# A two-block transformer step on one core: the low part of the stream moved beside its high part in the dense products

## The chip, the core and the metric

The kernel runs on one core of one Trainium2 chip. The core has a matrix engine (TensorE, PE in the profile, with its weight loads shown apart as PEld), a vector engine (VectorE, DVE), a scalar engine (ScalarE, ACT), a slower elementwise engine (GpSimd, POOL) and a queue that issues transfers (SyncE, SP). The metric is the device time of one execution in microseconds (us), median of several runs.

## The reference, cut to what matters

Two transformer blocks over 256 positions of width 1024, all in float32. The first has a layer of gated causal attention with 16 heads ("fox"), a feed-forward, a layer of latent attention with 8 heads ("mla") and a second feed-forward. The second has a mixer (a spatial gating unit beside differential attention), cross-attention into 256 memory tokens, and a mixture of 32 experts. The part that the change touches is a chain of dense products with a nonlinearity, such as

```python
def sq_relu_mlp(h, w_up, w_down):
    return jnp.square(jax.nn.relu(h @ w_up)) @ w_down

x = x + fox_mixer(rms_norm(x, g0), ...)        # q, k, v products, 16 heads, output product
x = x + sq_relu_mlp(rms_norm(x, g1), w_up, w_down)   # 1024 -> 4096 -> 1024, twice
x = x + mla_mixer(...)                          # low-rank products, 8 heads, output product
z = rms_norm(x, g2) @ w_in                      # second block: u, v, q, k and values
x = x + memory_attention(...)
x = x + hierarchical_moe(...)
```

## The kernel before, in words

The stream is held feature-major: 8 chunks of 128 features on the partitions, 256 positions in the free dimension. To keep float32 accuracy with fast products, every operand is split in two float32r parts: the high part is the value rounded to float32r, the low part is what the rounding left. A product of one weight block of 128x128 with one chunk of the stream is then three matmuls of 256 columns into the same 256 columns of a PSUM bank (`mm3`, L454 to L456): high weight with high stream, high weight with low stream, low weight with high stream.

The weights come as a planned sequence of slices. Most slices are 128x1024: eight 128x128 blocks that together give 128 output features, so eight `mm3` calls, 24 matmuls. A ring of SBUF tiles receives the slices by DMA; `prep` (L419, L425) splits a slice: ACT casts the high part (128x1024), DVE subtracts for the low part. `take` calls `prep` so that three slices ahead are split (`NSPLIT = 4`); the low part is issued one call late, at the next `prep` or `flush`. So the program order on ACT is, for each slice: cast of a later slice, then what evacuates this slice's PSUM bank; on DVE: subtraction of a later slice, then its share of the evacuation. Each engine runs its instructions in this program order.

`proj` takes one slice, draws one of the two banks tagged `pp`, issues its `mm3` calls and returns the bank. The caller evacuates it, in `fox` with one DVE multiplication by the row of reciprocal norms (L855, L859), in `ffn` with four instructions (L942 to L945): ACT relu, ACT square into the high part `hh`, DVE square, DVE subtraction into the low part `hl`. The third slice in a row has to wait until the first one's bank is evacuated.

The dense slices come in this order: 8 for the memory keys (mk), wide ones with 512 moving columns (mv, fv: `proj_wide`, L462 to L464, whose stationary operand is the stream), 16 for fox (fk, fq), 8 output (fo), then the feed-forward in four blocks of 8 `up` and 8 `down` slices; then qa 3, kva 3, kb, qn, qr, vb of mla, 8 output (mo), the second feed-forward; then sv (wide), su 4, dk and dq 4 each around a wide dv, 8 output (wo), 8 mq, 8 om. `out_proj` adds the bank of an output slice to the stream (`finish_x`, L917) and makes the next normalised operand from it (L513, L514).

Attention work is put between the slices by a small pipe: each `pipe.step()` issues the next stage of the heads under way (scores L641, softmax L597 and L599, normalise L606 or L1223 and L1225, transpose L612, values). In the `up` part of a block nothing but the slices runs. At the first `up` slice of a feed-forward the reciprocal norm is computed (L537 on PE, L573 and L575 on ACT, L578 to L580 and L556 on DVE) ahead of that slice's evacuation. In `second`, two ACT gelu instructions on `vt` (L1189) stand ahead of the evacuation of the first su slice.

The last third of the time is the mixture of experts, which reads three tiles of 128x4096 float32 for each expert.

Of the kernel before, what the change touches and what calls it, by code (L numbers as in the profile page):

```python
# [303 lines left out]

class Program:
# [151 lines left out]

    def mm3x(self, out, xh, xl, w, o, n, start, stop):
# [44 lines left out]
    def pair(self, name, n=8, pool=None):  # L503
        return tuple(self.t(name + part, [128, n, 256], F32R, pool=pool) for part in "hl")
# [201 lines left out]
    def memory_keys(self, memx):  # L706
# [14 lines left out]
        for m in range(8):  # L721
# [68 lines left out]
    def fox(self):  # L790
# [58 lines left out]
        for c in range(8):  # L849
# [8 lines left out]
            p = self.proj("fq", xn)  # L858
            nc.vector.scalar_tensor_tensor(q, p, 0.125, rb, op0=OP.mult, op1=OP.mult)  # L859
# [14 lines left out]
    def out_proj(self, key, ctx, norms, k2=0, order=range(8), post=None, mid=None, between=None, ahead=2):  # L874
# [3 lines left out]
        first = []  # L878
        if k2:
            oldest = self.used  # L880
            groups, n = k2 if isinstance(k2, tuple) else (k2,), 0
            for a, b in zip((0, *groups), groups):
                for m in range(ahead):
                    if a == 0:
                        first.append((self.bank("pp" if m < 2 else "ps", [128, 256]), self.take(key, oldest)))
                    p, w = first[m]
                    for i in range(a, b):
                        k = order[i]
                        self.mm3(p, w, k * 128, 128, ctx[0][:, k], ctx[1][:, k], i == 0, False)
# [6 lines left out]
        for m in range(8):  # L896
            if m < len(first):
                p, w = first[m]
            else:
                p, w = self.bank("pp", [128, 256]), self.take(key)  # L900
            for i in range(k2 if m < len(first) else 0, 8):
                k = order[i]
                self.mm3(p, w, k * 128, 128, ctx[0][:, k], ctx[1][:, k], i == 0, i == 7)
            if post and m > 1:
                post(m - 2)
            self.finish_x(m, p, norms, split=post and m == 7)
# [21 lines left out]
    def ffn(self, layer, norms, final=False):  # L928
# [6 lines left out]
        for b in range(4):  # L935
            for f in range(8):
# [17 lines left out]
            for m in TURNS if b == 3 else range(8):  # L954
# [7 lines left out]
                if b == 3:  # L962
                    t = self.t("rs", [128, 256], bufs=2)
                    nc.vector.tensor_mul(t, o, r2)
                    self.finish_x(m, t, [(n, self.nxt[n]) for n in self.nxt])
# [19 lines left out]
    def mla(self):  # L985
# [8 lines left out]
        for part in (range(0, 6), range(6, 8)):  # L994
            for c in range(3):
                if part[0] == 0:
                    late.append(self.bank("acc", [128, 256]))
# [887 lines left out]
```

## Time and profile before

| | before |
|---|---|
| median of 3 runs (lowest, highest) | 1271.92 us (1270.92, 1272.26) |
| the profiled execution's own time | 1270.38 us |
| its span, first to last instruction | 1268.7 us |
| PE busy, weight loads | 1198.2 us, 966.5 us |
| DVE busy, ACT busy, POOL busy | 661.2 us, 525.0 us, 156.0 us |
| DMA moved | 338.63 MB |

Busy times are unions of instruction intervals over the span. A matmul's interval is its latency, and consecutive matmuls overlap; the pace of PE is read from the starts of consecutive matmuls, not from their durations. "Idle before <- X" names what an engine's instruction waited for last.

### The profile page before, as it was taken

The page shows a single profiled execution, that of the slowest core. Times are in us where ns is not written, and L with a number is a line of the kernel's source. Part 1 is how long each engine was busy: PE and PEld are TensorE (multiplying, and loading weights), DVE is VectorE, ACT ScalarE, POOL GpSimd, SP SyncE. Part 2 cuts the span into 40 slices and gives each one's busy share as a digit, 9 for nine tenths or more (in the row PEclk, how much of TensorE's full clock was granted, in tenths as well). Part 3 has the DMA queues.
Part 4 walks back from the last instruction along what each step waited for, and adds up shares of the span by engine and source line. Part 5 has one row for each costly group of instructions (what it writes and reads, how often), then busy time and mean ns, then how long its engine had stood idle before and what let it go on. Part 6 is the DMA issues. An engine that isn't in the chain of part 4 may idle for free. (4 is left out here: it accounts for less than half of the span.)

```text
span 1268.7 us, 22238 instructions
## 1 busy us (share of the span) xinstructions
PE 1198.2 (94%) x9282; PEld 966.5 (76%) x9282; DVE 661.2 (52%) x1249; ACT 525.0 (41%) x980; POOL 156.0 (12%) x169
## 2 busy tenths in 40 slices
PE   8999999999999999999999999988999999787886
PEld 7788899999998899999998898854554545444333
DVE  7657675654787574654789775432222223222222
ACT  4555564544654664544665554221112122121212
POOL 5166110000032010000145110100000000000000
PEclk9999999999999999999999999998999999898997
DMA  9554435545442345544554358899999999999995
GB/s 347 198 211 153 169 133 200 192 163 204 173 165 94 133 142 192 199 169 172 191 211 184 134 199 346 318 378 427 424 426 425 427 424 425 427 424 425 426 421 205
DMA packets 30520, 338.63 MB, mean 267 GB/s; under 512 B 3521, under 2 KB 3793, under 8 KB 8401
## 3 DMA queue, kind: packets, MB, share of 16 engines
q1 hardware_dynamic: 30272, 336.92, 66.8%
q8 instruction: 74, 1.21, 0.4%
q10 hardware_dynamic: 144, 0.26, 0.1%
q14 instruction: 30, 0.24, 0.1%
HBM read 336.10 MB, written 1.06 MB: 266 GB/s over the span
## 5 line engine op out<-in xcount | busy, mean ns | idle before, releaser
L425 DVE TENSOR_TENSOR wl<-ring,wh 128x1024 fp32r<-128x1024 f32 (+1 forms) x244 | 302.9, 1246 | 73.6 <-ACT wh L419 73.6
L419 ACT CAST wh<-ring 128x1024 fp32r<-128x1024 f32 (+1 forms) x246 | 252.6, 1030 | 140.7 <-PE acc L455 95.8
L454 PE MATMUL pp<-xh,wh 128*128 128x256 f32 x800 | 227.3, 284 | 0.1
L455 PE MATMUL pp<-xl,wh 128*128 128x256 f32 x800 | 225.9, 282 | 0.4 <-DVE xl L514 0.4
L456 PE MATMUL pp<-xh,wl 128*128 128x256 f32 x800 | 225.9, 282 | 0.0
L455 PE MATMUL acc<-hl,wh 128*128 128x256 f32 x560 | 159.3, 284 | 1.6 <-DVE hl L514 1.0
L456 PE MATMUL acc<-hh,wl 128*128 128x256 f32 x560 | 158.5, 283 | 0.9 <-DVE wl L425 0.9
L454 PE MATMUL acc<-hh,wh 128*128 128x256 f32 x560 | 158.7, 283 | 0.0
L454 PEld LDWEIGHTS pp<-xh,wh 128*128 128x128 f32 x800 | 151.6, 189 | 2.2 <-issue 1.6
L455 PEld LDWEIGHTS pp<-xl,wh 128*128 128x128 f32 x800 | 150.3, 188 | 0.8 <-DVE xl L514 0.6
L456 PEld LDWEIGHTS pp<-xh,wl 128*128 128x128 f32 x800 | 150.1, 188 | 0.0
L1644 PE MATMUL pp<-ring,xg 128*32 128x512 f32 x1024 | 125.9, 627 | 21.2 <-DMA ring<-in_we_dram 18.3
L530 POOL TENSOR_TENSOR sq<-sq,sqt 128x256 f32<-128x256 f32 x58 | 47.1, 812 | 535.4 <-ACT sqt L528 534.6
L455 PEld LDWEIGHTS acc<-hl,wh 128*128 128x128 f32 x560 | 107.4, 192 | 3.3 <-DVE hl L514 3.3
L1648 DVE COPY gs<-pp 128x512 f32<-128x512 f32 x32 | 22.1, 692 | 166.7 <-PE pp L1644 166.7
L456 PEld LDWEIGHTS acc<-hh,wl 128*128 128x128 f32 x560 | 107.5, 192 | 1.1 <-DVE wl L425 1.1
L454 PEld LDWEIGHTS acc<-hh,wh 128*128 128x128 f32 x560 | 107.6, 192 | 0.7 <-ACT hh L513 0.7
L1644 PEld LDWEIGHTS pp<-ring,xg 128*32 128x32 f32 x1024 | 31.1, 113 | 97.0 <-issue 86.2
L1680 DVE TENSOR_TENSOR yl<-ps,yh 128x512 fp32r<-128x512 f32 x64 | 44.2, 691 | 77.1 <-ACT yh L1679 77.1
L1657 PEld LDWEIGHTS ps<-ca,gs 128*128 128x128 f32 x512 | 59.9, 191 | 24.8 <-issue 24.4
L1677 PE MATMUL ps<-ring,sh 128*32 128x512 f32 x512 | 67.7, 650 | 8.6 <-DVE sh L1667 4.7
L454 PE MATMUL pp<-hh,wh 128*128 128x256 f32 x248 | 72.2, 291 | 0.8 <-DVE x L917 0.8
(379 smaller groups left out, 1938.8 us busy)
## 6 DMA issues: line engine op xcount, KB each, us to landing
ring<-in_we_dram SPq DMA_DIRECT2D x76, 2048.0 KB, 29.8
ring<-in_wd_dram SPq DMA_DIRECT2D x58, 2048.0 KB, 8.1
ring<-in_we_dram SPq DMA_DIRECT2D x34, 1024.0 KB, 29.7
ring<-in_we_dram SPq DMA_DIRECT2D x12, 512.0 KB, 14.5
bc<-cdr SPq DMA_DIRECT2D x8, 256.0 KB, 6.5
ring<-in_wd_dram SPq DMA_DIRECT2D x1, 1792.0 KB, 7.6
ring<-in_wd_dram SPq DMA_DIRECT2D x1, 1536.0 KB, 9.9
pb<-in_pb_dram SPq DMA_DIRECT2D x1, 1152.0 KB, 10.8
```

The lines of the kernel that those rows point to most:

```text
L419: self.nc.scalar.copy(h[:, :n], w)
L425: eng.tensor_sub(l[:, :n], w, h[:, :n].bitcast(F32))
L454: mm(out, wh, xh, start=start, stop=False, skip_group_check=skip)
L455: mm(out, wh, xl, start=False, stop=False, skip_group_check=skip)
L456: mm(out, wl, xh, start=False, stop=stop, skip_group_check=skip)
L530: nc.gpsimd.tensor_add(total, total, tmp)
L1644: mm(p[32 * j:32 * j + 32], xg(k), w(k * 512, k * 512 + 512), start=k < 4, stop=k > 3, tile_position=(0, 32 * j))
L1648: v.tensor_copy(g, p)
L1657: mm(p[:, f], g[:, f * 128:f * 128 + 128], self.cst("fold"), start=True, stop=True)
L1677: mm(p[32 * j:32 * j + 32], h[:, j], w(o, o + 512), start=True, stop=True, tile_position=(0, 32 * j))
L1680: v.tensor_sub(yl[:, c], p, yh[:, c].bitcast(F32))
```

## The change

`pair` lays the high and the low part of one chunk side by side, as 512 contiguous columns. `mm2` multiplies a high weight block with both parts in one matmul of 512 columns, which fills a whole PSUM bank, and the low weight block with the high part in a second matmul of 256 columns into the right half. The bank then holds two halves that have to be added: `halves` copies the right one to SBUF on ACT and adds the left one on DVE. The output slices fo, mo and om add both halves to the stream by two DVE additions instead. In `up` the relu and the square are one DVE instruction on the sum, and the split into high and low is `hilo` (an ACT cast, a DVE subtraction). The mk slices are scaled by POOL after the addition; fq, qr, dk, dq and mq are treated as fk is shown below. The `down` slices, wo, qn, kb and the wide slices keep their products.

```diff
+class Half:
+    def __getitem__(self, key):
+        v = self.pair.both(key[1])[:, self.i]
+        return v[:, key[2]] if len(key) > 2 else v
+class Pair:
+    def both(self, k):
+        return self.tiles[k // self.n][:, k % self.n]
+    def __getitem__(self, i):
+        return Half(self, i)
...
+    def mm2(self, out, w, o, x, k, start, stop):
+        mm = self.nc.tensor.matmul
+        mm(out.rearrange("p (a b) -> p a b", b=256), w[0][:, o:o + 128], x.both(k), start=start, stop=stop,
+           skip_group_check=True)
+        mm(out[:, 256:], w[1][:, o:o + 128], x[0][:, k], start=False, stop=stop, skip_group_check=True)
+
+    def halves(self, dst, p):
+        self.nc.scalar.copy(dst, p[:, 256:])
+        self.nc.vector.tensor_add(dst, dst, p[:, :256])
+        return dst
...
     def proj(self, key, x, nk=8, order=None, banks="pp"):
         w = self.take(key)
-        p = self.bank(banks, [128, 256])
+        p = self.bank(banks, [128, 512])
         for i, k in enumerate(order or range(nk)):
-            self.mm3(p, w, k * 128, 128, x[0][:, k], x[1][:, k], i == 0, i == nk - 1)
+            self.mm2(p, w, k * 128, x, k, i == 0, i == nk - 1)
         return p
...
     def pair(self, name, n=8, pool=None):
-        return tuple(self.t(name + part, [128, n, 256], F32R, pool=pool) for part in "hl")
+        parts = "hl" if n > 4 else "h"
+        n //= len(parts)
+        return Pair([self.t(name + part, [128, n, 2, 256], F32R, pool=pool) for part in parts], n)
...
-                    nc.vector.tensor_mul(mk[:, i], b, rm)
+                    self.halves(mk[:, i], b)
+                    nc.gpsimd.tensor_mul(mk[:, i], mk[:, i], rm)
...
-            p = self.proj("fk", xn)
-            nc.vector.tensor_mul(k, p, rb)
+            self.halves(k, self.proj("fk", xn))
+            nc.vector.tensor_mul(k, k, rb)
...
-        nc.vector.tensor_add(x[:, m], x[:, m], add)
+        for part in add:
+            nc.vector.tensor_add(x[:, m], x[:, m], part)
...
-                nc.scalar.activation(a, p, AF.Relu)
-                nc.scalar.activation(hid[0][:, f], a, AF.Square)
-                nc.vector.tensor_mul(s, a, a)
-                nc.vector.tensor_sub(hid[1][:, f], s, hid[0][:, f].bitcast(F32))
+                self.halves(a, p)
+                nc.vector.scalar_tensor_tensor(s, a, 0.0, a, op0=OP.max, op1=OP.mult)
+                self.hilo(hid, f, s)
...
-                    self.mm3(late[c], ws[c], k * 128, 128, xn[0][:, k], xn[1][:, k], i == 0, i == 7)
+                    self.mm2(late[c], ws[c], k * 128, xn, k, i == 0, i == 7)
...
-            nc.vector.tensor_mul(z, p, rb)
+            nc.vector.tensor_mul(z, self.halves(z, p), rb)
...
-            nc.vector.tensor_mul(z2, late[c], rb)
+            nc.vector.tensor_mul(z2, self.halves(z2, late[c]), rb)
...
-            nc.vector.tensor_mul(ug[:, g], p, rb)
+            nc.vector.tensor_mul(ug[:, g], self.halves(ug[:, g], p), rb)
             nc.scalar.activation(ug[:, g], ug[:, g], AF.Gelu)
```

## Rows read from the trace of the kernel before

**Rows 1.** The page, busy us, share and instructions of two engines

```profile
PE 1198.2 (94%) x9282; PEld 966.5 (76%) x9282; DVE 661.2 (52%) x1249; ACT 525.0 (41%) x980; POOL 156.0 (12%) x169
```

**Rows 2.** Busy time by stretch: width, PE, PEld, DVE, ACT, POOL, clock, DMA, GB/s

```profile
225.00:250.00 25.00, 25.00 (x211) 25.00 (x210) 17.96 (x26) 14.98 (x25) 0.00 (x0) 1.00 0.40 148
...
660.00:700.00 40.00, 39.06 (x282) 34.79 (x281) 35.92 (x94) 24.42 (x53) 19.84 (x16) 1.00 0.43 158
...
900.00:1000.00 100.00, 94.39 (x781) 50.00 (x780) 26.62 (x59) 20.31 (x44) 0.00 (x0) 0.99 1.01 426
```

**Rows 3.** Timeline of PE, 256 moving columns: start us, us, engine, line

```profile
224.87 0.28 PE L454 MATMUL pp<-xh,wh 128*128 128x256 f32 x1
...
244.66 0.28 PE L454 MATMUL pp<-xh,wh 128*128 128x256 f32 x1
```

**Rows 4.** Timeline of PE, 512 moving columns, in mv and in fv

```profile
61.71 0.39 PE L464 MATMUL pp<-wl,hh 128*128 128x512 f32 x1
...
63.07 0.39 PE L464 MATMUL pp<-wl,hh 128*128 128x512 f32 x1
...
136.42 0.40 PE L464 MATMUL ps<-wl,xh 128*128 128x512 f32 x1
...
138.53 0.40 PE L464 MATMUL ps<-wl,xh 128*128 128x512 f32 x1
```

**Rows 5.** Timelines of ACT, DVE and PE at the last up slice of a block

```profile
245.22 0.38 ACT L942 ACTIVATE ra<-pp 128x256 f32<-128x256 f32 x1 [1.11 <-PE pp L456]
245.64 0.42 ACT L943 ACTIVATE hh<-ra 128x256 fp32r<-128x256 f32 x1
...
246.17 0.43 DVE L945 TENSOR_TENSOR hl<-rs,hh 128x256 fp32r<-128x256 f32 x1
...
245.03 0.28 PE L454 MATMUL acc<-hh,wh 128*128 128x256 f32 x1
```

**Rows 6.** Timeline of DVE where it never waits

```profile
340.25 0.42 DVE L964 TENSOR_TENSOR rs<-acc,rb 128x256 f32<-128x256 f32 x1 [0.37 <-PE acc L456]
340.70 0.42 DVE L917 TENSOR_TENSOR x<-x,rs 128x256 f32<-128x256 f32 x1
341.05 1.22 DVE L425 TENSOR_TENSOR wl<-ring,wh 128x1024 fp32r<-128x1024 f32 x1
342.19 0.48 DVE L514 SCALAR_TENSOR_TENSOR xl<-x,pa,xh 128x256 fp32r<-128x256 f32 x1
```

**Rows 7.** First block of a feed-forward: PE's second up slice, first evacuation, first down

```profile
178.61 0.47 PE L454 MATMUL pp<-xh,wh 128*128 128x256 f32 x1
...
181.67 0.42 DVE L944 TENSOR_TENSOR rs<-ra 128x256 f32<-128x256 f32 x1
...
198.95 0.28 PE L454 MATMUL acc<-hh,wh 128*128 128x256 f32 x1
```

**Rows 8.** PE's two waits in mla

```profile
380.06 0.38 PE L455 MATMUL acc<-cnl,wh 128*128 128x256 f32 x1 [1.03 <-DVE cnl L514]
...
390.49 0.35 PE L454 MATMUL pp<-qnh,wh 128*128 128x256 f32 x1 [1.02 <-DVE qq L1086]
```

**Rows 9.** ACT ahead of the first su evacuation, and PE's third su slice

```profile
658.35 1.28 ACT L1189 ACT_TABLE_LOAD   x1 [2.00 <-DVE r L1164]
...
660.80 1.04 ACT L419 CAST wh<-ring 128x1024 fp32r<-128x1024 f32 x1
661.74 0.42 ACT L1194 ACTIVATE ug<-ug 128x256 f32<-128x256 f32 x1
...
660.43 0.36 PE L454 MATMUL pp<-xh,wh 128*128 128x256 f32 x1
```

**Rows 10.** PE's scores and transposes between the dk and dq slices

```profile
675.26 0.93 PE L641 MATMUL acc<-fk,fq 64*128 64x128 f32 x8
...
683.22 0.84 PE L612 MATMUL acc<-ca,P 128*128 128x128 f32 x3 [0.24 <-DVE P L1225]
...
691.09 0.83 PE L612 MATMUL acc<-ca,P 128*128 128x128 f32 x3 [0.50 <-DVE P L1225]
```

More of the change, by code (lines that the diff above doesn't have):

```diff
@@ L302, in drain, with __init__ @@
             self.step()
+class Half:
+    def __init__(self, pair, i):
+        self.pair, self.i = pair, i
+    def __getitem__(self, key):
+        v = self.pair.both(key[1])[:, self.i]
+        return v[:, key[2]] if len(key) > 2 else v
+class Pair:
+    def __init__(self, tiles, n):
+        self.tiles, self.n = tiles, n
+    def both(self, k):
+        return self.tiles[k // self.n][:, k % self.n]
+    def __getitem__(self, i):
+        return Half(self, i)
 class Program:
@@ L853, in fox @@
             k = self.t("fk", [128, 256], bufs=3)
-            p = self.proj("fk", xn)
-            nc.vector.tensor_mul(k, p, rb)
+            self.halves(k, self.proj("fk", xn))
+            nc.vector.tensor_mul(k, k, rb)
             pipe.step()
             q = self.t("fq", [128, 256], bufs=3)
-            p = self.proj("fq", xn)
-            nc.vector.scalar_tensor_tensor(q, p, 0.125, rb, op0=OP.mult, op1=OP.mult)
+            self.halves(q, self.proj("fq", xn))
+            nc.vector.scalar_tensor_tensor(q, q, 0.125, rb, op0=OP.mult, op1=OP.mult)
             pipe.step()
@@ L878, in out_proj, with unit @@
         first = []
+        merged = key != "wo"
+        width = 512 if merged else 256
+        def unit(p, w, k, start, stop):
+            if merged:
+                self.mm2(p, w, k * 128, ctx, k, start, stop)
+            else:
+                self.mm3(p, w, k * 128, 128, ctx[0][:, k], ctx[1][:, k], start, stop)
         if k2:
@@ L884, in out_proj @@
                     if a == 0:
-                        first.append((self.bank("pp" if m < 2 else "ps", [128, 256]), self.take(key, oldest)))
+                        first.append((self.bank("pp" if m < 2 else "ps", [128, width]), self.take(key, oldest)))
                     p, w = first[m]
@@ L888, in out_proj @@
                         k = order[i]
-                        self.mm3(p, w, k * 128, 128, ctx[0][:, k], ctx[1][:, k], i == 0, False)
+                        unit(p, w, k, i == 0, False)
                         n += 1
@@ L899, in out_proj @@
             else:
-                p, w = self.bank("pp", [128, 256]), self.take(key)
+                p, w = self.bank("pp", [128, width]), self.take(key)
             for i in range(k2 if m < len(first) else 0, 8):
                 k = order[i]
-                self.mm3(p, w, k * 128, 128, ctx[0][:, k], ctx[1][:, k], i == 0, i == 7)
+                unit(p, w, k, i == 0, i == 7)
             if post and m > 1:
                 post(m - 2)
-            self.finish_x(m, p, norms, split=post and m == 7)
+            self.finish_x(m, [p[:, i:i + 256] for i in range(0, width, 256)], norms, split=post and m == 7)
             if post and m == 3:
@@ L964, in ffn @@
                     nc.vector.tensor_mul(t, o, r2)
-                    self.finish_x(m, t, [(n, self.nxt[n]) for n in self.nxt])
+                    self.finish_x(m, [t], [(n, self.nxt[n]) for n in self.nxt])
                     if final:
@@ L996, in mla @@
                 if part[0] == 0:
-                    late.append(self.bank("acc", [128, 256]))
+                    late.append(self.bank("acc", [128, 512]))
                     ws.append(self.take("qa", oldest))
@@ L1092, in mla @@
             z = self.t("z", [128, 256], bufs=2)
-            nc.vector.scalar_tensor_tensor(z, p, scale, rq, op0=OP.mult, op1=OP.mult)
+            nc.vector.scalar_tensor_tensor(z, self.halves(z, p), scale, rq, op0=OP.mult, op1=OP.mult)
             keys(2 * p2 + 2)
@@ L1316, in second @@
             k = self.t("fk", [128, 256], bufs=2)
-            p = self.proj("dk", xn)
-            nc.vector.tensor_mul(k, p, rb)
+            nc.vector.tensor_mul(k, self.halves(k, self.proj("dk", xn)), rb)
             if h == 3:
@@ L1327, in second @@
             q = self.t("fq", [128, 256], bufs=2)
-            p = self.proj("dq", xn)
-            nc.vector.scalar_tensor_tensor(q, p, 0.125, rb, op0=OP.mult, op1=OP.mult)
+            self.halves(q, self.proj("dq", xn))
+            nc.vector.scalar_tensor_tensor(q, q, 0.125, rb, op0=OP.mult, op1=OP.mult)
             if h == 3:
@@ L1411, in memory @@
                     rb = self.rstd(D, rows=True)[0]
-                nc.vector.scalar_tensor_tensor(q[:, c], p, 1.0 / 16.0, rb, op0=OP.mult, op1=OP.mult)
+                self.halves(q[:, c], p)
+                nc.vector.scalar_tensor_tensor(q[:, c], q[:, c], 1.0 / 16.0, rb, op0=OP.mult, op1=OP.mult)
                 pipe.step()
```

## The prediction

> **What bounds the kernel now.** I read the page first, then busy time by stretch, the timelines of PE, DVE and ACT in one slice of each kind, and last PE's waits. The page has PE busy for 94% of the span against 52% for DVE and 41% for ACT [rows 1]. Whether PE sets the pace everywhere is seen from the stretches. In a feed-forward PE never rests while DVE works 17.96 of 25 us; around su, dk and dq PE is nearly full too, but DVE works 35.92 of 40 us [rows 2]: there little fits on DVE any more. From 900 us on the DMA share is 1.01 and PE waits for expert weights [rows 2]; what the dense part gains or loses earlier moves the start of that part, and with it the end, one for one.
>
> PE's pace is not the 0.28 us of a matmul. From 224.87 to 244.66 us stand 55 groups of three matmuls [rows 3]: 0.360 us a group, 0.120 a matmul, 2.88 a slice of 8 groups. Matmuls with 512 columns follow each other at 1.36/6 = 0.2267 us in mv and 2.11/9 = 0.2344 us in fv [rows 4].
>
> **PE's part of the change.** A group becomes one matmul of 512 columns and one of 256. 138 slices of 8 groups and four qr slices of 3 make 1116 groups. The pair isn't in the trace. Its upper bound is 0.2344 + 0.120 = 0.3544 us; its lower one 0.2267 + 0.1133 = 0.340, if the 256-column half also goes at half the mv row. I take 0.351, between the two rows of 512 and with the full 0.120, as both are loads of weights followed by a stream. That saves 0.009 a group, 0.07 a slice (2.81), and 10.0 us if PE alone counted (6.2 to 22.3 by the bounds). The clock is 1.00 in the dense stretches [rows 2], so nothing is to be had from it.
>
> The Trainium skill ("TensorE: Matmul & The Clock Gate", section "Back-to-back issue gap") puts an isolated gap at N/2.4 + 2.5 ns, so that joining two matmuls saves 2.5 ns; by it 1116 groups would give 2.8 us in place of 10.0. The trace has 120 ns where that formula has 109, and 227 to 234 where it has 216, so the rows are used.
>
> **What the halves cost.** ACT copies a half (0.38 us, as the relu from the same bank [rows 5]), DVE adds the other 0.04 later. On DVE a dependent instruction of 256 columns starts 0.45 after the one before it, an independent one 0.35 after, and what follows a weight subtraction 1.14 after [rows 6]. Where one DVE instruction evacuated a bank, there are now an ACT copy, an addition and the old instruction on its result: 0.45 us more on DVE, 0.83 more until the result, and the copy stands in ACT's order behind the cast of a later slice and whatever came before.
>
> *Slices that can hide it.* In mk, fox, fo, mo, mq and om (56 slices) nothing after the slice needs the result at once, and mk trades a multiplication on DVE for the addition. The cover is DVE's idle time, which a feed-forward stretch puts at 7 of 25 us [rows 2]; without it, 56 x 0.45 = 25 us would show. I count PE's saving in full: 56 x 0.07 = 4.0 us gained.
>
> *Up slices, blocks two to four of both feed-forwards.* DVE's program per slice becomes: addition, 0.45; square, 0.42 + 0.04; wait for the ACT cast, 0.42 + 0.03; subtraction to next, 0.35; weight subtraction, 1.14: 2.85 us, 0.04 over PE's 2.81. After seven slices DVE is 0.3 late. The last low part is then ready 0.38 + 0.04 + 0.45 + 0.46 + 0.45 + 0.43 + 0.3 = 2.5 us after 245.22, at 247.7, where now it is at 246.6 [rows 5]. The down slice that starts at 245.03 [rows 5] wants it after seven groups and a matmul, at 247.67. So 0.1 is lost of 0.56: 0.46 x 6 = 2.8 us gained. If the wait for ACT is 0.11, as the subtraction shows now behind the square (246.17 after 246.06 [rows 5]), the loop is 2.93 and a block loses 0.1 instead.
>
> *The first block of each feed-forward.* DVE comes to the first evacuation only at 181.67, because the reciprocal norm is ahead of it, while PE is in its second slice since 178.61 [rows 7]. Now DVE catches up, with 1.8 us of work a slice. With a loop of 2.85 it can't: the eighth addition starts at 181.67 + 7 x 2.85 = 201.6, its low part is ready 1.8 later, at 203.4. PE wants it at 198.95 + 2.64 = 201.6 [rows 7]. Late: the down slices, by 1.8, twice: 3.6 us lost. Bounds: 0, if PE's third slice were the only one to wait and DVE caught up; 5, with the loop of 2.93.
>
> *mla.* PE waits for DVE at 380.06 and 390.49 [rows 8], so additions ahead of these count in full. Before the first stand three (kva, qa, kva): 3 x 0.45, and 0.15 for a copy: 1.5. Before the second stand three more, part of them beside DVE's present wait for the norm: 0.9. The qr slice has one before the rotation that PE takes next: 0.6. Sum 3.0 us lost; bounds 1.5 (the first wait alone) and 4.
>
> *su, dk, dq.* Here the copy is late by ACT's order. The table load at 658.35, two gelus and a cast stand ahead of the first su evacuation; the cast starts at 660.80, the next ACT instruction at 661.74 [rows 9]. The copy takes that place: bank free at 661.74 + 0.42 + 0.42 = 662.6. PE's third su slice, which draws this bank, starts now at 660.43 [rows 9]: 2.2 us later. Then PE isn't given it back: the nine additions from the second su to the third dq slice are 9 x 0.42 = 3.8 us on DVE, and 35.92 + 3.8 = 39.7 of 40 leaves no room. Behind it: the copy of the last dk or dq stands on ACT behind four exponentials (1.9 us) and a cast, DVE's normalising behind that copy's addition, and PE's transposes, which wait for DVE at 683.22 and 691.09 already [rows 10], behind the normalising. The scores at 675.26 [rows 10] I put 3.3 us later, the transposes about 6.5, and after 692 wide matmuls fill PE, so the delay stays: 6.5 us lost. Bounds: 2.2 and 9.
>
> *Five short places.* An addition (0.45) lies on the path from fo and from mo into the first up slice (0.2 each, the rest is slack), at the last dq (0.4), the last mq (0.75 with the copy) and the last om, on the way to the router (0.45): 2.0 us lost, bounds 0 and 2.6.
>
> **The sum.** Gained 4.0 + 2.8 = 6.8; lost 3.6 + 3.0 + 6.5 + 2.0 = 15.1; net 8.3 us longer. The profiled execution took 1270.38 us, span 1268.7, and lies 1.5 under the median of the runs shown. 1270.38 + 8.3 = 1278.7; against the median 1271.92 + 8.3 = 1280.2. I predict 1280 us.
>
> **The rivals.**
> *The waits stay where they arise.* DVE and ACT each have over 40% of the span idle [rows 1]; if mla costs 1.5 and su 2.2, the first blocks 1.8, the sum is 1.8 + 1.5 + 2.2 + 2.0 - 6.8 = +0.7: 1272.6. Against it: DVE at 90% from 660 to 700 [rows 2]. Chance 0.17, half of it within 0.2%.
> *The pair is faster and the end comes earlier.* Place: the 448 groups of the 56 slices where PE alone sets the pace (up slices can't follow, DVE's loop takes 2.85). Price: 4.5 us for every 10 ns of the pair. It decides from 0.351 - 8.3/448 = 0.3325 us; at 0.32 it gives 13.9 more, and the time is 1266.3. For it: a third of the weight loads goes, and they are 76% busy [rows 1]. Against it: 512 columns alone take 0.2267, and half of that is 0.113 [rows 4]. Chance 0.05; with the case that copies and additions all hide, 1261.9, it is 0.13.
> *The pair saves next to nothing.* At 0.3544 a slice saves 0.045 instead of 0.07, over 56 + 48 slices 4.7 instead of 6.8: 1282.3. Chance 0.10. By the formula of the Trainium skill named above a slice would save 0.02, the gains would be 2.1 and the time 1284.9; the trace, at 120 and 227 to 234 ns, doesn't agree with it.
> *The up loop is 2.93.* Six blocks lose 0.1 instead of gaining 0.46, the first blocks 1.4 more together: 4.8 more, 1285.0. For it: the 0.11 [rows 5]. Chance 0.15.
> The forecast, 1276 to 1284, has 0.45.
>
> **How the numbers follow.** A measurement here tells 0.2%, about 2.5 us, from no change. Faster: 0.13 and a little of the first rival, 0.15. Same: 0.10. Slower: 0.75. For 8 in 10 the range goes down to 1266, which leaves the cases where everything hides, and up to 1287, past the slower loop; the likeliest case's own range is 1276 to 1284.
>
> **What the profile after would show.** Right: pairs 0.351 us apart in blocks two to four; DVE's additions in `up` 2.85 apart and the down slices of a first block some 2 us behind; PE idle ahead of the third su slice, released by DVE's addition, and ahead of the transposes; the waits at kb and qn longer by 1.5 and 2.4. Wrong: a pair under 0.335; DVE catching up in the first block; no wait at the third su slice.

## The result, and the profile after

| | before | after |
|---|---|---|
| median, beside each other | 1272.02 us | 1282.73 us (1281.68 to 1284.65, 4 runs) |
| ratio, with its 95% interval | | 1.0088 (1.0075 to 1.0100) |
| the profiled execution's own time, span | 1270.38, 1268.7 us | 1281.68, 1279.9 us |

The change makes the kernel 0.9% slower, 10.7 us by the medians. The page of the kernel after, for [rows 1], and its busy time in the stretches of [rows 2]:

```profile
PE 1190.7 (93%) x8166; PEld 906.9 (71%) x8166; DVE 714.3 (56%) x1383; ACT 539.5 (42%) x1034; POOL 169.5 (13%) x177
```

```profile
225.00:250.00 25.00, 25.00 (x157) 22.38 (x156) 19.85 (x34) 14.87 (x25) 0.00 (x0) 1.00 0.41 153
660.00:700.00 40.00, 34.23 (x180) 28.31 (x179) 31.74 (x86) 22.94 (x49) 19.32 (x18) 0.91 0.29 105
900.00:1000.00 100.00, 94.39 (x796) 50.16 (x792) 27.11 (x60) 20.31 (x44) 0.00 (x0) 1.00 1.01 425
```

PE has 1116 matmuls and 7.5 us of busy time less, and the kernel is longer all the same: between 660 and 700 us PE was busy for 39.06 us and is now for 34.23, and the clock there is 0.91. The two windows don't hold the same work, as su now starts 6.3 us later (660.85 us in place of 654.51). From the start of su to the start of wo DVE worked 47.85 of 55.30 us before and works 49.42 of 61.99 after: it has a little more to do, in a smaller share of the time. What is added there is mostly waiting.

PE's timeline in an up slice of the second block (L486 is the matmul of 512 columns, L488 that of 256), for [rows 3]:

```profile
223.74 0.39 PE L486 MATMUL pp<-xh,wh 128*128 128x512 f32 x1
223.97 0.28 PE L488 MATMUL pp<-xh,wl 128*128 128x256 f32 x1
...
226.54 0.39 PE L486 MATMUL pp<-xh,wh 128*128 128x512 f32 x1
```

Eight pairs from 223.74 to 226.54 us: 0.350 us a pair. DVE's timeline in the same block (L493 is the addition, L995 the square, L548 the low part, L449 the weight subtraction), for [rows 6]:

```profile
226.09 0.42 DVE L493 TENSOR_TENSOR ra<-ra,pp 128x256 f32<-128x256 f32 x1 [3.93 <-ACT ra L492]
226.55 0.42 DVE L995 SCALAR_TENSOR_TENSOR rs<-ra 128x256 f32<-128x256 f32 x1
227.44 0.43 DVE L548 TENSOR_TENSOR hh<-rs,hh 128x256 fp32r<-128x256 f32 x1 [0.47 <-ACT hh L547]
227.79 1.22 DVE L449 TENSOR_TENSOR wl<-ring,wh 128x1024 fp32r<-128x1024 f32 x1
...
234.57 0.42 DVE L493 TENSOR_TENSOR ra<-ra,pp 128x256 f32<-128x256 f32 x1
```

Three loops from 226.09 to 234.57: 2.83 us each, beside 2.80 of PE. The wait for ACT is 0.47, near the 0.45 that the prediction's loop had, not the 0.11 of its rival.

**A ledger by stage.** In each trace I took the start of the first product matmul of every stage from PE's rows, subtracted its start in the first profile of before, and then took what each stage adds to that difference. A positive number is time lost in that stage. The kernels are those of the next section; "up 2-4" is blocks two to four with their down slices. All in us:

| stage | after | pe_alone | cost_alone | no_copy | quiet_pool | apart_sudkdq | apart_block0 | apart_fomo | apart_mla | only_gains |
|---|---|---|---|---|---|---|---|---|---|---|
| fox | -0.85 | -0.85 | 0.00 | -0.85 | -0.87 | -0.85 | -0.85 | -0.85 | -0.85 | -0.88 |
| fo | -0.42 | -0.42 | 0.00 | -0.42 | -0.42 | -0.42 | -0.42 | 0.00 | -0.42 | 0.00 |
| first block, 1st feed-forward | +2.74 | -0.55 | +2.34 | +2.72 | +1.99 | +2.72 | +0.84 | +1.76 | +2.75 | 0.00 |
| up 2-4, 1st | -1.61 | -1.84 | 0.00 | -1.84 | -1.61 | -1.66 | -1.67 | -1.63 | -1.62 | -1.67 |
| qa, kva | -0.04 | -0.25 | +0.01 | -0.23 | -0.03 | -0.04 | -0.05 | -0.01 | +0.08 | +0.09 |
| kb | +3.87 | +0.06 | +3.85 | +3.37 | +3.69 | +3.93 | +5.20 | +3.90 | 0.00 | +0.01 |
| qn, qr | +0.87 | -0.03 | +0.77 | +0.61 | +1.03 | +0.82 | +0.55 | +0.83 | +0.04 | -0.01 |
| mo | +0.24 | -0.12 | +0.33 | +0.28 | -0.12 | +0.31 | +0.34 | 0.00 | +0.34 | +0.01 |
| first block, 2nd | +3.95 | -0.55 | +3.64 | +3.95 | +1.97 | +3.88 | +1.99 | +1.77 | +4.34 | 0.00 |
| up 2-4, 2nd | -1.61 | -1.84 | 0.00 | -1.84 | -1.64 | -1.67 | -1.63 | -1.65 | -1.62 | -1.64 |
| su | +3.26 | -0.06 | +1.95 | -0.02 | +3.36 | +0.02 | +1.81 | +1.81 | +3.38 | 0.00 |
| dk, dq | +3.44 | +0.53 | +4.40 | +1.89 | +3.44 | 0.00 | +4.36 | +4.37 | +3.42 | 0.00 |
| wo, mq | +0.63 | -0.35 | +1.00 | -0.08 | +0.65 | +0.31 | +0.62 | +0.65 | +0.62 | -0.03 |
| sum, fox to mq | +14.46 | -6.28 | +18.28 | +7.52 | +11.43 | +7.34 | +11.08 | +10.94 | +10.45 | -4.12 |

The first column is the result in short: fox, fo and the up parts of blocks two to four gain 4.5 us; the first blocks lose 6.7, mla (kb, qn, qr) 4.7, and su, dk and dq 6.7.

The medians don't show the whole sum. The whole change is 10.7 us longer by them and not 14.5, pe_alone 9.8 shorter and not 6.3, and in the other five kernels with several executions they lie 1.0 to 2.7 us under the sum. The mk slices, ahead of fox, can account for 0.6 of it (8 slices at 0.07). Where the rest comes back, before fox or from om on, no run here settles. So the ledger says which stage loses what, and the medians what the kernel gains or loses.

### The profile page after: what moved, and what is told of

Its sections match the earlier page's. It is cut to its first block, busy times and chain, and to the rows that moved or that the text cites. A ratio compares the mean times of both kernels' runs of the same rounds, so it can differ in the third digit from the quotient of the medians.

```text
span 1279.9 us, 20067 instructions
## 1 busy us (share of the span) xinstructions
PE 1190.7 (93%) x8166; PEld 906.9 (71%) x8166; DVE 714.3 (56%) x1383; ACT 539.5 (42%) x1034; POOL 169.5 (13%) x177
## 5 line engine op out<-in xcount | busy, mean ns | idle before, releaser
L449 DVE TENSOR_TENSOR wl<-ring,wh 128x1024 fp32r<-128x1024 f32 (+1 forms) x244 | 301.4, 1242 | 68.1 <-ACT wh L443 68.1
L443 ACT CAST wh<-ring 128x1024 fp32r<-128x1024 f32 (+1 forms) x246 | 253.8, 1033 | 109.6 <-PE acc L479 78.9
L486 PE MATMUL pp<-xh,wh 128*128 128x512 f32 x400 | 150.2, 407 | 3.1 <-DVE ug L493 2.4
L486 PE MATMUL pp<-xl,wh 128*128 128x512 f32 x400 | 145.2, 395 | 3.3 <-DVE xl L554 3.3
L570 POOL TENSOR_TENSOR sq<-sq,sqt 128x256 f32<-128x256 f32 x58 | 47.3, 815 | 527.0 <-ACT sqt L568 524.7
L488 PE MATMUL pp<-xh,wl 128*128 128x256 f32 x400 | 113.1, 283 | 0.0
L488 PE MATMUL pp<-xl,wl 128*128 128x256 f32 x400 | 111.7, 279 | 0.0
L486 PEld LDWEIGHTS pp<-xh,wh 128*128 128x128 f32 x400 | 76.2, 191 | 22.9 <-DVE ug L493 2.7
L486 PEld LDWEIGHTS pp<-xl,wh 128*128 128x128 f32 x400 | 75.3, 188 | 22.2 <-DVE xl L554 4.3
L488 PEld LDWEIGHTS pp<-xh,wl 128*128 128x128 f32 x400 | 76.4, 191 | 0.2
L488 PEld LDWEIGHTS pp<-xl,wl 128*128 128x128 f32 x400 | 75.2, 188 | 0.0
L480 PE MATMUL acc<-hh,wl 128*128 128x256 f32 x256 | 72.4, 283 | 0.0
L478 PE MATMUL acc<-hh,wh 128*128 128x256 f32 x256 | 72.4, 283 | 0.0
## 6 DMA issues: line engine op xcount, KB each, us to landing
ring<-in_we_dram SPq DMA_DIRECT2D x12, 512.0 KB, 14.5
```

The source lines that it names most:

```text
L443: self.nc.scalar.copy(h[:, :n], w)
L449: eng.tensor_sub(l[:, :n], w, h[:, :n].bitcast(F32))
L478: mm(out, wh, xh, start=start, stop=False, skip_group_check=skip)
L480: mm(out, wl, xh, start=False, stop=stop, skip_group_check=skip)
L486: mm(out.rearrange("p (a b) -> p a b", b=256), w[0][:, o:o + 128], x.both(k), start=start, stop=stop, skip_group_check=True)
L488: mm(out[:, 256:], w[1][:, o:o + 128], x[0][:, k], start=False, stop=stop, skip_group_check=True)
```

## The experiments

Each begins from the changed kernel, but for the second look at the kernel before.

**How much of a stage's time is scatter.** The kernel before, profiled again.

> The kernel before, profiled once more, for the scatter of single stages. Theory (the experts' part of the changed kernels, 1.8 to 4 us shorter than the first profile's 446.1 us from its first matmul to the end of the span, is scatter between executions): 442 to 446 us here, mostly below the first profile; the start of mk and of fox within 1.5 us of the first profile. Rival (the change itself shortens that part, because its transfers stand differently when the dense part ends): 446 us again.

1270.72 us. From the start of fox to the start of om, over 600 us, no stage differs from the first profile by more than 0.02 us. The scatter sits at both ends: the time until fox (0.92 longer), om (1.54 longer), and the experts' part: 443.95 us, where the first profile has 446.13 and the changed kernels lie from 441.95 (apart_mla) to 446.69 (filled_kb), quiet_pool aside. The rival's 446 again did not come, and a changed kernel had 446.69. So the theory holds as far as one more profile can tell: the 2.5 us that the first comparison seemed to give back (13.7 late at the start of the experts' part, 11.3 at the end of the span) need no other cause than scatter. By the second profile the experts start 11.26 us later after the change and the span ends 10.97 later. Hence the ledger, and not one execution's time, decides below where a single stage is in question.

**The two sides of the change.** pe_alone keeps the pairs and evacuates the left half alone, as the kernel before evacuates a bank (what the right half holds is left out); cost_alone keeps three products and pays for two halves.

```diff
 def halves(self, dst, p):                                 # pe_alone
-    self.nc.scalar.copy(dst, p[:, 256:])
-    self.nc.vector.tensor_add(dst, dst, p[:, :256])
-    return dst
+    return p[:, :256]
...
 def mm2(self, out, w, o, x, k, start, stop):              # cost_alone
-    mm(out.rearrange(...), w[0][:, o:o + 128], x.both(k), ...)
-    mm(out[:, 256:], w[1][:, o:o + 128], x[0][:, k], ...)
+    self.mm3(out[:, :256], w, o, 128, x[0][:, k], x[1][:, k], start, stop)
 def halves(self, dst, p):
-    self.nc.scalar.copy(dst, p[:, 256:])
-    self.nc.vector.tensor_add(dst, dst, p[:, :256])
+    self.nc.scalar.copy(dst, p[:, :256])
+    self.nc.vector.tensor_max(dst, dst, p[:, :256])
```

> All 138 slices and qr keep the joined pair, but what evacuates a bank reads only its left half, with the instructions of the kernel before; the part of the product that the right half holds is left out of the results. Theory (pair 0.351 us, 1116 groups): the start of the experts' part 8 to 10 us earlier than before, all of it from slices where PE sets the pace, and no new wait ahead of the first up slices, the third su slice, kb or qn; ratio 0.992 to 0.994. Rival (the pair is worth less, and the 0.60 us an up block gained is DVE's new order): 2.8 us, ratio 0.998.

> All groups stay three products of 256 columns into one half of a bank; after each slice ACT copies that half and DVE joins it with the same half once more (a maximum, or in fo, mo and om an addition of zero times it), so that the evacuations take as long as in the change. Theory (prediction's losses, less what a PE slice of 2.88 us in place of 2.81 gives DVE to catch up with): 13 to 16 us over the kernel before, ratio 1.0102 to 1.0126; su, dk, dq 6 us and mla 4.5 us of it, up blocks two to four nothing. Rival (the pair makes no wait longer, so the costs are the whole change's 10.7 plus PE's 10): 20 to 24 us, ratio 1.016 to 1.019.

pe_alone: 1263.04 against 1272.86 us, ratio 0.9927 (0.9913 to 0.9942). Every one of the eight up parts gains 0.54 to 0.61, and no new wait shows at the places that the theory names; one of 1.74 us does among dk and dq, where PE waits for GpSimd (685.80 us). By the median, 9.8 us, PE's part is what the prediction took. By the ledger only 6.3 us arrive between fox and om, and the experts start 5.4 us earlier than in the first profile of before, 7.9 earlier than in the second: mo gains only 0.12, and mla, su, dk and dq gain nothing, as a faster PE waits longer there. The rival falls. cost_alone: 1289.76 us, ratio 1.0134 (1.0120 to 1.0149), that is 15 to 19 us, above most of the theory's band and under the rival's. su, dk and dq (6.35) and mla (4.62) cost what the theory said, and up 2-4 nothing; the first blocks cost 6.0, more than the prediction had for them. In the ledger the costs are about three times the gain (18.3 and 6.3 us), by the medians 1.7 times (16.9 and 9.8). The two sides make 18.3 - 6.3 = 12.0 in the ledger, the whole change 14.5: together they cost more. Most of the difference lies in the first blocks (6.0 - 1.1 = 4.9 against 6.7); that PE's shorter slice leaves DVE nothing to catch up with there is my reading, which no run tries by itself.

**One stage undone at a time.** In each the named slices go back to `mm3`, a bank of 256 columns and the old evacuation; all but apart_fomo share the edit of the first two pairs of lines. The expectations count a wait from the start of one matmul to the start of the next, 0.27 or 0.28 us more than the idle time in the rows (2.29 and 2.02 us ahead of the first up slice of the second feed-forward).

```diff
-        p = self.bank(banks, [128, 512])
+        joined = key not in self.apart
+        p = self.bank(banks, [128, 512 if joined else 256])
...
-            self.mm2(p, w, k * 128, x, k, i == 0, i == nk - 1)
+            if joined:
+                self.mm2(p, w, k * 128, x, k, i == 0, i == nk - 1)
+            else:
+                self.mm3(p, w, k * 128, 128, x[0][:, k], x[1][:, k], i == 0, i == nk - 1)
...
+    apart = ('su', 'dk', 'dq')                            # apart_sudkdq
+    apart = ('qa', 'kva', 'qr')                           # apart_mla
+                self.apart = self.apart + ("up",) if b == 0 else type(self).apart   # apart_block0
-        merged = key != "wo"
+        merged = key not in ('wo', 'fo', 'mo')            # apart_fomo
```

> Only su, dk and dq go back to three products. Theory (the copy in ACT's order and a full DVE cost this stage 6.5 us by the prediction, 6.7 by the positions in the two traces, and nothing later hides them): 4 to 5 us over the kernel before, ratio 1.0032 to 1.0042; no wait of 2.6 us ahead of the third su slice. Rival (the stage only hands on a delay that wo, mq or the experts would have waited for anyway): the end comes back by under 2.5 us, ratio 1.0068 or more.

> Only qa, kva and qr go back to three products. Theory (additions ahead of the waits at kb and qn count in full): the start of qn, and with it of mo, 4.5 us earlier than with the whole change, and the waits at kb and qn as before. Rival (prediction's size): 3.0 us. Second rival (the waits come from the norms of kva and qa, whose order on ACT changed with the up slices before them): under 1.5 us.

> Only the up slices of the first block of each feed-forward go back to three products. Theory (prediction: DVE starts this block late and its loop of 2.83 us can't catch up, so the first down slice waits): the waits of 1.25 us ahead of the first down slices and of 0.66 at the third up slice go, the waits ahead of the first up slice (1.08 and 2.29 us) stay, since fo and mo make them; the end 3.3 to 3.6 us earlier than with the whole change, 7.5 to 8 us over the kernel before, ratio 1.006. Rival (the whole delay of these blocks, the wait ahead of the first up slice too, is of their own additions): 6.7 us earlier, ratio 1.0035.

> Only fo and mo go back to three products and one addition. Theory formed on the trace after (two additions, the low part beside GpSimd's running sum and a weight subtraction fill DVE in these slices, so its lag at their start is carried into the feed-forward): the waits ahead of the first up slices (1.08 and 2.29 us) go, the end comes 3 us earlier than with the whole change, 8 us over the kernel before, ratio 1.0063. Rival (the prediction's 0.2 us for each of these places, the waits being of the copy and the addition in up): the end is within 1 us of the whole change, 11 to 12 us over the kernel before, ratio 1.009, as PE's gain of 1.1 us in these 16 slices goes too.

apart_sudkdq: 1277.56 against 1271.63 us, ratio 1.0053 (1.0038 to 1.0068); su, dk and dq cost 0.02 us in place of 6.70. The theory's 1.0032 to 1.0042 lies at the lower end of the interval, the rival's 1.0068 at its upper end; in the ledger 7.1 of 14.5 us go, and the profiled span ends 5.2 us earlier than with the whole change, so the rival's 2.5 falls. apart_mla (1277.03 us, one execution): kb and qn, qr cost 0.04 in place of 4.74: the theory, not the first rival's 3.0 or the second's 1.5.

apart_block0 (1281.70 us, ratio 1.0083, 1.0066 to 1.0099): the first blocks lose 2.83 in place of 6.69, so their own additions cost 3.9. What stays are waits ahead of the first up slice:

```profile
176.84 0.39 PE L479 MATMUL pp<-xl,wh 128*128 128x256 f32 x1 [0.62 <-DVE xl L562]
...
463.06 0.38 PE L478 MATMUL pp<-xl,wh 128*128 128x256 f32 x1 [0.43 <-ACT xl L561]
464.52 0.38 PE L479 MATMUL pp<-xl,wh 128*128 128x256 f32 x1 [1.07 <-DVE xl L562]
```

By the medians it can't be told from the whole change. The theory's ratio of 1.006 and the rival's 1.0035 both lie under the interval. In the ledger it is 3.4 us better from fox to mq, as the theory had it; the rival's 6.7 falls. That sum is in part chance: of the 3.9, kb takes back 1.3 and dk, dq 0.9, and su gives 1.4 (the granted clock, below, bears on kb and su). apart_fomo (1279.93 us, ratio 1.0068, 1.0053 to 1.0082): the first blocks lose 3.53 in place of 6.69, so fo and mo cause 3.2 us of it, which the theory had and its rival (11 to 12 us over before) had not.

**Why fo and mo cost so much.** quiet_pool leaves out GpSimd's running sum of squares in fo and mo.

```diff
+        if quiet:                                         # key in ("fo", "mo")
+            self.sq = self.t("sq", [128, 256], bufs=2)
+            nc.scalar.activation(self.sq, x[:, m], AF.Square)
-        if split:
+        elif split:
```

> The whole change, but in fo and mo the squares aren't summed up on GpSimd (each overwrites the last, so that the norm behind them comes of the last chunk alone). Theory (DVE's low part takes 0.96 us in place of 0.48 because GpSimd's sum of 0.74 us runs beside it, which makes DVE's loop 2.80 us, as long as PE's slice, so that DVE's lag is carried to the first up slice): low parts at 0.48, a loop of DVE's own work of 2.3 us, the waits ahead of the first up slices 1.08 and 2.29 fall to under 0.5, the first up blocks together at least 2 us shorter. Rival (the second addition alone does it, GpSimd's sum is only beside it): low parts still 0.9 us or more and the waits within 0.3 us of 1.08 and 2.29.

Timelines of POOL, DVE and PE in mo, the whole change (L969 adds the two halves, L449 subtracts weights, L554 makes the low part, L570 is GpSimd's sum):

```profile
455.93 0.74 POOL L570 TENSOR_TENSOR sq<-sq,sqt 128x256 f32<-128x256 f32 x1 [2.06 <-ACT sqt L568]
...
455.99 0.97 DVE L554 SCALAR_TENSOR_TENSOR xl<-x,pa,xl 128x256 fp32r<-128x256 f32 x1
456.88 0.86 DVE L969 TENSOR_TENSOR x<-x,pp 128x256 f32<-128x256 f32 x2
457.66 1.22 DVE L449 TENSOR_TENSOR wl<-ring,wh 128x1024 fp32r<-128x1024 f32 x1
458.79 0.96 DVE L554 SCALAR_TENSOR_TENSOR xl<-x,pa,xl 128x256 fp32r<-128x256 f32 x1
...
465.40 0.50 PE L486 MATMUL pp<-xl,wh 128*128 128x512 f32 x1 [2.02 <-DVE xl L554]
```

and DVE's in quiet_pool:

```profile
457.58 0.48 DVE L554 SCALAR_TENSOR_TENSOR xl<-x,pa,xl 128x256 fp32r<-128x256 f32 x1
...
460.83 0.88 DVE L970 TENSOR_TENSOR x<-x,pp 128x256 f32<-128x256 f32 x2 [0.42 <-PE pp L488]
```

In the whole change DVE's loop is 2.80 us (455.99 to 458.79), as long as PE's slice, so that whatever DVE is late at the start of mo is still late at its end, where PE's first up slice waits 2.02. Without the sum the low part takes 0.48, DVE catches up and waits for PE (0.42), and both waits ahead of the first up slices are gone; the two first blocks lose 3.96 in place of 6.69, which is 2.7 of the 3.2 us that apart_fomo put down to fo and mo. The rival falls. (With other norms behind fo and mo the experts' part took 32 us longer, 1314.20 us in all; only the ledger is used.)

**Copy or addition.** no_copy takes ACT's copy out and keeps a DVE instruction of the addition's size (the right half is left out, but for fo, mo and om).

```diff
 def halves(self, dst, p):
-    self.nc.scalar.copy(dst, p[:, 256:])
-    self.nc.vector.tensor_add(dst, dst, p[:, :256])
+    self.nc.vector.tensor_mul(dst, self.ones, p[:, :256])
```

> The whole change without ACT's copies: DVE's addition becomes a product of the left half with a tile of ones, of the same size and place, which waits for PE alone; the right half is left out of the results (fo, mo and om still add both). Theory (in su the bank comes free late because the copy stands behind the table load, two gelus and a cast on ACT; in dk and dq DVE's additions fill DVE): the wait of 2.63 us ahead of the third su slice falls under 0.6, su costs under 0.8 in place of 3.3, dk and dq together still 2 to 4 us; kb 3.5 to 3.9 and the first blocks within 0.4 us of the whole change, as DVE's additions set these. Rival A (the additions alone make the wait in su): su still 2.5 us or more. Rival B (the copies make most waits): kb under 2 us and the first blocks at least 1 us shorter each.

1277.04 us. Timelines of ACT, DVE and PE at the third su slice of the whole change (L1240 is the gelu on `vt`, L443 a cast, L492 the copy, L493 the addition), for [rows 9]:

```profile
665.98 1.26 ACT L1240 ACTIVATE vt<-acc,r 128x512 f32<-128x512 f32 x2
667.14 1.04 ACT L443 CAST wh<-ring 128x1024 fp32r<-128x1024 f32 x1
668.07 0.38 ACT L492 COPY ug<-pp 128x256 f32<-128x256 f32 x1
...
668.49 0.42 DVE L493 TENSOR_TENSOR ug<-ug,pp 128x256 f32<-128x256 f32 x1 [2.20 <-ACT ug L492]
...
668.96 0.79 PE L486 MATMUL pp<-xh,wh 128*128 128x512 f32 x1 [2.35 <-DVE ug L493]
```

and PE's in no_copy:

```profile
666.63 0.47 PE L486 MATMUL pp<-xh,wh 128*128 128x512 f32 x1 [0.15 <-ACT vt L1239]
```

In su the copy, late by its place in ACT's order, makes the whole cost (3.26 to -0.02). Part of that is the granted clock, which fell behind the wait: where the wait is the same and the clock stayed at 1.00, in apart_fomo and apart_block0, su costs 1.81. In dk and dq the copy makes 1.55 of 3.44, at wo and mq 0.71. In kb it makes 0.5 of 3.87 and in the first blocks nothing: there DVE's extra instruction costs. Timelines of DVE and PE at a dq slice of the whole change (L1379 scales dq, L681 are scores, L652 transposes), for [rows 10]:

```profile
692.40 0.42 DVE L493 TENSOR_TENSOR fq<-fq,pp 128x256 f32<-128x256 f32 x1 [1.10 <-ACT fq L492]
...
693.66 0.93 PE L681 MATMUL acc<-fk,fq 64*128 64x128 f32 x8 [1.73 <-DVE fq L1379]
695.68 1.08 PE L652 MATMUL acc<-ca,P 128*128 128x128 f32 x3 [1.10 <-DVE P L1276]
```

ACT runs four exponentials and a cast ahead of that copy (from 689.30 us, the copy at 692.01), DVE's addition waits for the copy, and PE's scores and transposes wait for DVE: the chain that the prediction gave. The theory holds in kind at each of these places (kb at 3.37 and dk, dq at 1.89 lie just under its figures), and both rivals fall: su went, and kb and the first blocks stayed.

**The clock at kb.** PE's waits at kb, for [rows 8], and what follows them:

```profile
380.00 0.38 PE L478 MATMUL acc<-cnh,wh 128*128 128x256 f32 x1 [2.23 <-ACT cnh L553]
381.46 0.39 PE L479 MATMUL acc<-cnh,wh 128*128 128x256 f32 x1 [1.07 <-DVE cnh L554]
...
382.21 0.42 PE L478 MATMUL acc<-cnh,wh 128*128 128x256 f32 x1
382.42 0.41 PE L479 MATMUL acc<-cnh,wh 128*128 128x256 f32 x1
```

```profile
382.00:384.00 2.00, 2.00 (x12) 2.00 (x11) 1.31 (x4) 1.34 (x4) 0.73 (x1) 0.51 0.00 0
384.00:386.00 2.00, 2.00 (x12) 1.95 (x12) 1.39 (x5) 0.96 (x3) 0.00 (x1) 0.63 0.00 0
```

After the waits the granted clock is 0.51 and 0.63, the lower of its two levels (1.2 GHz) for most of that time, and matmuls stand 0.21 apart, not 0.12. The Trainium skill ("TensorE: Matmul & The Clock Gate", section "Back-to-back issue gap") gives N/1.2 ns for that level, 213 for 256 columns; the trace agrees. From 382.03 to 385.41 PE takes 16 steps, 3.38 us in place of 16 x 0.12 = 1.92: 1.5 us more. Two kernels fill the waits with matmuls of ones.

```diff
                 for k in range(2):
+                    if g == 0 and h == 0 and k == 1:
+                        fill = self.bank("ps", [128, 256])
+                        for _ in range(16):               # 8 in filled_kb8
+                            nc.tensor.matmul(fill, self.ones[:, :128], self.ones, start=True, stop=True)
```

> The whole change, and 16 matmuls of ones into an unused bank between the third and the fourth matmul of kb, where PE waits 2.5 and 1.5 us. Theory (kb's 3.87 us are 2.4 us of longer waits and 1.5 us of a granted clock of 0.51 to 0.63 behind them, which comes of PE's idle time): the clock stays at 1.00 from 380 to 388, the matmuls that stood 0.213 us apart go back to 0.12, kb costs 2.2 to 2.6 us. Rival (the clock falls for another reason, or the extra matmuls delay the fourth): 3.8 us or more.

> The whole change with 8 matmuls of ones in the wait at kb in place of 16: each ran as two passes, 0.22 us a pass (32 passes took 7.07 us and kept the fourth kb matmul waiting until 384.4), so 8 take 3.5 us of the 4.0 that PE waits there. Theory (1.5 of kb's 3.87 us are the clock that falls behind the waits): granted clock 1.00 from 380 to 388, kb's 256-column matmuls 0.12 apart, kb 2.2 to 2.6 us longer than before. Rival (the clock is not what the waits cost): 3.6 us or more with the clock at 1.00.

In filled_kb (1286.40 us) the clock stayed at 1.00, but the filling itself took until 384.4 and kb cost 5.46: it settles nothing about the price. filled_kb8 (1284.42 us), its stretches and PE's next wait:

```profile
382.00:384.00 2.00, 2.00 (x19) 2.00 (x18) 1.31 (x4) 1.35 (x4) 0.69 (x1) 1.00 0.00 0
384.00:386.00 2.00, 2.00 (x16) 1.89 (x16) 1.39 (x4) 0.84 (x3) 0.05 (x1) 1.00 0.00 0
```

```profile
387.81 0.67 PE L577 MATMUL ps<-sq,ones 128*128 128x256 f32 x2 [0.85 <-DVE ln L618]
```

The clock is 1.00, yet kb costs 3.47, and qn, qr 1.25 in place of 0.87: together 4.72 against 4.74. PE arrives earlier at the sum for qa's norm, and waits there for a step of kva's norm on DVE. My theory falls, though 3.47 lies between its 2.6 and the rival's 3.6: without the slow clock kb is 0.4 shorter and qn, qr 0.4 longer, as DVE's chain sets the end of the two with it or without it. This holds for the whole change only. In apart_block0 PE waits just as long at kb (2.23 and 1.07 us), but the granted clock is 0.52 from 380 to 386 us, and kb costs 5.20; from there on PE runs to qn without another wait, so in that run the slow clock seems to be on the path, which no run tries.

**What is left when only the gains are kept.** The pair stays in mk, fox and the up slices of blocks two to four.

```diff
+    apart = ('qa', 'kva', 'qr', 'su', 'dk', 'dq', 'mq')
+                self.apart = self.apart + ("up",) if b == 0 else type(self).apart
-        merged = key != "wo"
+        merged = key not in ('wo', 'fo', 'mo', 'om')
```

> The joined pair is kept in mk, in fox and in the up slices of blocks two to four; every other slice goes back to three products and one evacuating instruction. Theory (pair 0.351 us against a group of 0.360, copies and additions hidden in these stages alone): 56 x 0.07 falls to 24 x 0.07 = 1.7 in mk and fox plus 6 x 0.46 to 0.6 = 2.8 to 3.6 in the up blocks, so 4.5 to 5.5 us under the kernel before, ratio 0.9957 to 0.9965, with the start of the experts' part 4.5 to 6 us earlier. Rival A (the experts' part is bound by transfers that don't follow the dense part): its start is earlier but the end is not, ratio 0.999 to 1.001. Rival B (the gains of the joined stages were only catching up on waits made elsewhere): start and end within 2 us of before.

1264.82 against 1271.63 us, ratio 0.9952 (0.9938 to 0.9967): faster than both kernels. The ledger has -4.12 us from fox to mq, all from fox and the six up blocks, and no stage loses more than 0.09. Both rivals fall; this is the version to keep.

## Why the prediction was right, and where its terms were not

Slower was right, and so was the range; the net of 8.3 us was 2.4 to 2.7 short (10.7 by the medians, 10.97 by the second profile of before). That the total is this near is in part luck: the stages from fox to mq cost 14.5 us, and some of it comes back outside them, which no run here explains. Term by term, with the ledger of the whole change:

- *The pair, 0.351 us*: 0.350. By the formula for an isolated gap that the prediction cites from the Trainium skill ("TensorE: Matmul & The Clock Gate", section "Back-to-back issue gap") it would be 216 + 109 = 325 ns, an estimate; the trace of the pair doesn't agree with it.
- *Up slices of blocks two to four, -2.8*: -3.22. The loop is 2.83, not 2.85, and an up part gains 0.60; the down slices lose 0.06.
- *First blocks, +3.6*: right. With fo and mo apart they lose 1.76 and 1.77 us, predicted 1.8 each. DVE's additions start 2.82 apart from the late start on and never catch up; its last one and what PE waits for, for [rows 7]:

```profile
180.57 0.41 DVE L493 TENSOR_TENSOR ra<-ra,pp 128x256 f32<-128x256 f32 x1
...
200.33 0.42 DVE L493 TENSOR_TENSOR ra<-ra,pp 128x256 f32<-128x256 f32 x1
...
201.70 0.38 PE L478 MATMUL acc<-hl,wh 128*128 128x256 f32 x1 [0.98 <-ACT hl L547]
```

- *su, dk, dq, +6.5*: +6.70, and the mechanism of su, the copy's place in ACT's order, is shown by no_copy. The prediction took the clock as 1.00, and of su's 3.26 us 1.45 came with the clock behind the wait, a cost that it had no term for. In dk and dq the copy has 1.55 of the cost, the addition 1.89, and the chain from the copy to the transposes is the one predicted. That DVE would be full there was wrong (49.42 of 61.99 us from su to wo): it waits for ACT's copy in between.
- *From fo and mo into the first up slice, 0.2 each*: 3.2. This step failed most. The prediction called the rest of the addition slack; there is none, since GpSimd's sum doubles the low part's time and DVE's loop is then as long as PE's slice (quiet_pool, for 2.7 of the 3.2).
- *mla, +3.0*: +4.7. The place was right, the chain behind it longer. Timelines of POOL and DVE at the first kva evacuation after the change (L1059 multiplies by the norm):

```profile
369.07 6.01 POOL L449 TENSOR_TENSOR wl<-ring,wh 128x1024 fp32r<-128x1024 f32 x2 [4.31 <-ACT wh L443]
...
372.72 0.41 DVE L493 TENSOR_TENSOR z<-z,pp 128x256 f32<-128x256 f32 x1
373.16 2.20 DVE L1059 TENSOR_TENSOR z<-z,rb 128x256 f32<-128x256 f32 x1
```

and before it:

```profile
369.98 6.01 POOL L425 TENSOR_TENSOR wl<-ring,wh 128x1024 fp32r<-128x1024 f32 x2 [4.58 <-ACT wh L419]
...
373.63 0.41 DVE L1008 TENSOR_TENSOR z<-pp,rb 128x256 f32<-128x256 f32 x1
374.62 1.66 DVE L514 SCALAR_TENSOR_TENSOR cnl<-z,pa,cnh 128x256 fp32r<-128x256 f32 x1 [0.58 <-ACT cnh L513]
```

  Both stretched instructions end 0.28 or 0.29 us after GpSimd's weight subtraction (375.08 and 375.99). Before, the evacuation read PSUM and got through beside it, and only the low part was held; now the multiplication works on two SBUF tiles and is held, with everything after it still to come. That, and not the clock (filled_kb8), is where I see the missing 1.7 us; it was read from these rows, not tried by taking GpSimd's subtraction away.
- *Slices that can hide it, and the last places at dq, mq and om*: without mk 48 x 0.07 = 3.4 gained and 1.6 lost, -1.8; the ledger has -0.85 (fox), -0.42 (fo), +0.24 (mo), +0.63 (wo, mq) and +0.06 (om): -0.34. mo gains little even with its evacuation left as it was (pe_alone -0.12). mk lies in the scatter.

The differences are 2.8 (fo, mo), 1.7 (mla), 1.5 (hiding slices), 0.2 (su, dk, dq), -0.4 (up), -0.1 (first blocks) and -0.2 (until fox): 5.5, and 8.3 + 5.5 = 13.8 is what the experts' part starts later than in the first profile (13.73). Against the second profile that start is 11.26 later, so 2.5 us of it can't be told from scatter; from there to the end of the span the delay stays, 10.97, so that "one for one" holds against that profile. Of the rivals, the waits staying where they arise, a faster pair, the pair saving nothing and the loop of 2.93 all fell with the rows above.

## What to carry to other kernels

Price a change of the dense product at its evacuation first: where another engine's chain is on the path, every added instruction counts in full, and the place of a short copy in an engine's order can cost more (3.3 us in su, 1.8 where the clock did not fall) than the copy (0.38). Apply such a change slice by slice, and keep it only where nothing waits for the result: that turned +0.9% into -0.5%. When one engine's own timeline repeats to 0.02 us between executions, a ledger of stage starts shows differences of 0.1 us that medians with a scatter of several us can't. It doesn't say what makes them (the clock alone moved su by 1.45 us between kernels), and its sum is not the change of the whole time.

## What the hardware showed that I had not expected

- A DVE instruction that reads two SBUF tiles was held here while GpSimd worked: 0.97 us for the low part beside a sum of 0.74, 0.48 without it, 2.20 for a multiplication of otherwise 0.43 beside a weight subtraction; the addition between them in the timeline, with one operand in PSUM, took 0.41. The Trainium skill ("SBUF — State Buffer", section "Who interferes with whom") states this: such an instruction contends with a GpSimd instruction that reads SBUF, and whichever comes second waits. The trace agrees, with the 0.28 us from GpSimd's end to DVE's. In mla the change makes such an instruction out of one that read PSUM. In mo the low part read two SBUF tiles before too, but began 0.32 us ahead of GpSimd's sum (455.57 and 455.89 us) and took 0.48; the second addition puts it 0.06 behind.
- The clock fell behind PE's waits in some kernels and not in others. Behind a wait of 2.35 us at the third su slice, in the whole change and in apart_fomo:

```profile
667.00:670.00 3.00, 1.04 (x3) 0.94 (x4) 1.48 (x4) 2.05 (x5) 0.00 (x0) 0.80 0.00 0
670.00:673.00 3.00, 3.00 (x13) 2.52 (x13) 2.81 (x5) 2.05 (x4) 0.00 (x0) 0.64 0.47 98
```

```profile
667.00:670.00 3.00, 3.00 (x19) 2.64 (x18) 2.81 (x5) 2.05 (x4) 0.00 (x0) 1.00 0.42 82
670.00:673.00 3.00, 3.00 (x19) 2.60 (x18) 2.81 (x5) 2.05 (x5) 0.00 (x0) 1.00 0.96 399
```

  su costs 3.26 us in the one and 1.81 in the other, but dk and dq then 3.44 and 4.37: of 1.45 us only 0.52 is left when wo starts. In apart_block0 the clock stayed at 1.00 at this place and fell further than in the whole change at kb. What decides whether the clock falls stays open.
- Each matmul of float32 tiles (the ones) left two rows in the trace: 16 matmuls left 32 rows and took 7.07 us, 0.44 us a matmul of 256 columns where the float32r ones stand 0.12 apart.
